# Conditioning rows in pieces as large as a pass, in places of their own, and weights in three raw buffers

## The chip, the cores and the metric

One core of a Trainium2 chip runs the whole kernel. The metric is the time of one execution on the device in microseconds (us). Engines are named as in the profile: PE is TensorE (matmuls), DVE is VectorE, ACT is ScalarE, POOL is GpSimd, SP is SyncE, which only issues DMAs here.

## What is computed

One decoder layer for 256 tokens of width 2048 in float32: a SwiGLU feed-forward, a pair of token mixers side by side (chunkwise retention and sliding-window attention), a second SwiGLU, and a final norm. Each of the three parts is modulated by nine vectors that come from one conditioning row `c`:

```python
c_act = jax.nn.silu(c)
for l in range(DEPTH):
    mod = (c_act @ w_ada[l] + b_ada[l]).reshape(b, N_MOD, D_MODEL)
    h = modulate(rms_norm(x, norm_ffn1[l]), mod[:, 0], mod[:, 1])
    x = x + 0.5 * mod[:, 2][:, None, :] * swiglu(h, w_ffn1_gu[l], w_ffn1_down[l])
    h = modulate(rms_norm(x, norm_mix[l]), mod[:, 3], mod[:, 4])
    x = x + mod[:, 5][:, None, :] * token_mixing(h, w_in[l], ...)
    h = modulate(rms_norm(x, norm_ffn2[l]), mod[:, 6], mod[:, 7])
    x = x + 0.5 * mod[:, 8][:, None, :] * swiglu(h, w_ffn2_gu[l], w_ffn2_down[l])
return rms_norm(x, norm_final)
```

The change concerns how `w_ada` (9 x 2048 rows of 2048 numbers, transposed on the host) is read, and how the large weights share buffers with it.

## The kernel before

**Weights.** Every product is made of three TensorE passes on split operands. A weight tile (`raw`, 128 x 4 x 512, 1 MB) is loaded by SyncE (`load`, line 348). Each half of it, 128 x 1024 numbers, is cast by ScalarE to the high part `wh` (line 373), and VectorE writes the remainder `wl` (line 374). Both turn in three buffers (`wsp`). A half feeds twelve matmuls (lines 365 to 367): two slices of the contraction, two halves of the tokens, three products each. In the down products and the branch products the activations are split on the fly as well (`a`, lines 405 and 406). The pool `raws` has four buffers (`RAWS`).

**Conditioning.** The nine vectors are not made on TensorE, except for the first columns: VectorE multiplies a row of `w_ada` (128 x 2048, 1 MB) by `cact` and sums along the row (`ada_pass`, line 244). Such a pass covers a part of the row. Three sets run in the shadow of the products: the first (vectors 2, 4 and 3) beside the end of the first feed-forward, two passes of 1024 for each of 48 rows; the second (7, 6 and 5) beside the mixers, four passes of 512 for each of 48 rows; the third (8) beside the second feed-forward, four passes for each of 16 rows.

**What sets the order.** `conditioning` (line 283) is a generator; `tick`, called once after the products of each half (line 423), moves it on by the rate that `set_pace` worked out (for the second set 192 steps over 262 - 8 halves). A row is loaded whole, when the step two ahead of its first pass is reached. In the first set it goes into one of two places in a slot (`two_rows`); in the second and third it takes one of the four raw buffers (`raw_row`), beside the weights. SyncE's instructions stand in the order in which the program is written, and it works them off one after another, so a load that waits for its buffer holds those behind it. On TensorE, VectorE and ScalarE a scheduler sets the order from the program's priorities and its own model of time, except in a few stretches that are written out by hand: the start, and the ends of the three down products (`down_product`, line 642) with the norm that follows.

Of the kernel before, what the change touches and what calls it, by code (L numbers as in the profile page):

```python
# [10 lines left out]
F32 = mybir.dt.float32  # L11
# [6 lines left out]
P = 128  # L18
S = 256
D = 2048  # L20
DFF = 5632
NT = S // P
KD = D // P
KF = DFF // P
CH = 512
KB = 4
EPS = 1e-6
RAWS = 4
# [50 lines left out]
def layer_kernel(  # L79
# [23 lines left out]
    nc = tc.nc  # L103
    ctx.enter_context(tc.manual_schedule(engines={mybir.EngineType.SP}))
    b_ada = b_ada[0]
    one = ctx.enter_context(tc.tile_pool(name="one", bufs=1))
    raws = ctx.enter_context(tc.tile_pool(name="raws", bufs=RAWS))
    wsp = ctx.enter_context(tc.tile_pool(name="wsp", bufs=3))
    asp = ctx.enter_context(tc.tile_pool(name="asp", bufs=2))
    slots = ctx.enter_context(tc.tile_pool(name="slots", bufs=4))  # L110
# [9 lines left out]
    def nm(s):  # L120
        uid[0] += 1
        return f"{s}_{uid[0]}"
# [15 lines left out]

    def slot():
        return slots.tile([P, KD * S], F32, tag="slot", name=nm("slot"))  # L140

    def small(n, tag):
        return two.tile([P, n], F32, tag=tag, name=nm(tag))
# [88 lines left out]
    AQ = 4  # L232
    LEAD = 3

    def ada_load(m, k, w, loads=1):
        src = w_ada[(m * KD + k) * P : (m * KD + k + 1) * P, :]
        for i in range(loads):
            at = slice(i * D // loads, (i + 1) * D // loads)
            nc.sync.dma_start(w[:, at], src[:, at])

    def ada_pass(k, w, sums, q, passes=AQ):

        at = slice(q * D // passes, (q + 1) * D // passes)
        nc.vector.tensor_tensor_reduce(  # L244
            out=w[:, at],
            in0=w[:, at],
            in1=cact[:, at],
            scale=1.0,
            scalar=0.0,
            op0=ALU.mult,  # L250
            op1=ALU.add,
            accum_out=sums[:, k, q : q + 1],
        )

    def ada_sums():
        return two.tile([P, KD, AQ], F32, tag="sums", name=nm("sums"))

    def ada_end(m, ks, sums, i=None, passes=AQ):

        dest, total = modc[:, m, ks], sums[:, ks, 0]  # L260
        if passes > 1:
            total = dest
            nc.vector.tensor_reduce(out=dest, in_=sums[:, ks, :passes], axis=AX.X, op=ALU.add)
        nc.vector.tensor_add(dest, total, bcols[:, m, ks])
        if i is not None:
            nc.vector.tensor_mul(dest, dest, gains[:, i, ks])

    def raw_row():
        raw = raws.tile([P, KB, CH], F32, tag="raw", name=nm("raw"))
        return raw.rearrange("p k n -> p (k n)")  # L270

    def two_rows():

        both = slot()
        turn = [both[:, :D], both[:, D:]]

        def place():
            turn.append(turn.pop(0))
            return turn[-1]

        return place

    def conditioning(outputs, place, ahead, passes):


        tiles = [(m, k) for m, _, _ in outputs for k in range(KD)]
        held = {}
        step = 0
        for m, gain, row in outputs:
            sums = ada_sums()  # L290
            for k in range(KD):
                for q in range(passes):
                    for i in range(step // passes, min((step + ahead) // passes + 1, len(tiles))):
                        if i not in held:
                            held[i] = place()
                            ada_load(*tiles[i], held[i])
                    ada_pass(k, held[step // passes], sums, q, passes)
                    step += 1
                    if k == KD - 1 and q == passes - 1:
                        ada_end(m, slice(0, KD), sums, gain, passes)  # L300
                        if row is not None:
                            gate_out(m, row)
                    yield

    def gate_out(m, row):

        ps = bank()
        nc.tensor.transpose(ps[:KD, :P], modc[:, m, :], ident)
        flat = t512()[:KD, :P]
        nc.scalar.mul(flat, ps[:KD, :P], row)  # L310
        nc.gpsimd.dma_start(gate_d[m // 3].rearrange("(k p) -> k p", p=P), flat)
# [9 lines left out]

    pace = {"steps": iter(()), "rate": 0.0, "due": 0.0}

    def set_pace(outputs, halves, place, ahead, idle=0, passes=AQ):
        assert next(pace["steps"], None) is None
        pace["steps"] = conditioning(outputs, place, ahead, passes)
        pace["rate"] = len(outputs) * KD * passes / (halves - idle)
        pace["due"] = -idle * pace["rate"]

    def tick():  # L330
# [15 lines left out]


    def load(w, kb, c0):
        raw = raws.tile([P, KB, CH], F32, tag="raw", name=nm("raw"))
        nc.sync.dma_start(  # L350
            raw,
            w[kb * KB * P : (kb + 1) * KB * P, c0 : c0 + CH].rearrange(
                "(k p) n -> p k n", p=P
            ),
        )
        return raw
# [278 lines left out]
    def ffn_up(held, w, tiles, first, bg=None, ready=None):  # L635
        for ci in range(first, DFF // CH):
            bg = bg or gemm(held, w, [ci * CH])[0]
            bu = gemm(held, w, [DFF + ci * CH], ready=ready)[0]
            swiglu_up(bg, bu, tiles, ci)
            bg = ready = None  # L640

    def down_product(act, w, gate, KT, before, after):
# [12 lines left out]
        with tc.manual_schedule(engines=ORDERED):  # L655
# [11 lines left out]
            def late_pieces(kb):  # L667
                raw, place = load(w, kb, c0s[1]), home_tile()
                for h in range(2):
                    late[kb, h] = Piece(raw, h, place, h).both()  # L670
# [175 lines left out]
    early = [ada_sums() for _ in range(2)]  # L846
    rows_of = {}
# [4 lines left out]
    def place(m, k, loads=1):  # L852
        if k < 1:
            rows_of[m, k] = raw_row()
        elif k == 2:
            rows_of[m, k] = lead_rows.pop(0)
        else:
            ring.append(ring.pop(0))
            rows_of[m, k] = ring[-1]
        if (m, k) not in by_column:  # L860
            ada_load(m, k, rows_of[m, k], loads)
            return
        src = ada_first[by_column.index((m, k))]
        for i in range(loads):
            at = slice(i * D // loads, (i + 1) * D // loads)
            nc.sync.dma_start(rows_of[m, k][:, at], src[:, at])
# [4 lines left out]
    def order_of(g):  # L871
        return chunks if (g + len(groups)) % 2 else chunks[::-1]

    def block_of(n, k0, k1):
        c0 = (n % 2) * DFF + (n // 2) * CH
        return gu[k0 * P : k1 * P, c0 : c0 + CH]

    def lead_blocks(k):
        raw = raws.tile([P, KB, CH], F32, tag="raw", name=nm("raw"))
        for i, n in enumerate(order_of(0)[:LEAD]):  # L880
            nc.sync.dma_start(raw[:, i, :], block_of(n, k, k + 1))
        return raw

    def load_blocks(n, ks):
        raw = raws.tile([P, KB, CH], F32, tag="raw", name=nm("raw"))
        nc.sync.dma_start(
            raw[:, : len(ks), :],
            block_of(n, ks[0], ks[-1] + 1).rearrange("(k p) n -> p k n", p=P),
        )
        return raw  # L890
# [7 lines left out]
    place(1, 0, 2)  # L898
    place(0, 0, 4)
    lead = [lead_blocks(0)]  # L900
    place(1, 1)
    place(0, 1, 4)
# [3 lines left out]

    def passes_of(m, k, passes):
        for q in range(passes):
            ada_pass(k, rows_of[m, k], early[m], q, passes)

    def end_of(m, ks, passes):
        ada_end(m, slice(ks[0], ks[-1] + 1), early[m], 0 if m else None, passes)
# [130 lines left out]
    coming_raws, sent = {}, [0]  # L1043
# [15 lines left out]
    with tc.manual_schedule(engines=ORDERED):  # L1059
# [28 lines left out]
        def rounds(m, k, i0=0, i1=KD):  # L1088
# [8 lines left out]
            out=s2, in_=ssq.rearrange("p (t i) -> p t i", t=NT), axis=AX.X, op=ALU.add  # L1097
        )
        nc.vector.tensor_scalar(
            out=v2, in0=s2, scalar1=1.0 / D, scalar2=EPS, op0=ALU.mult, op1=ALU.add  # L1100
# [6 lines left out]
            out=q2, in0=q2, scalar1=-0.5, scalar2=1.5, op0=ALU.mult, op1=ALU.add  # L1107
# [75 lines left out]
    turn = [acc_bank, side_bank, acc_bank]  # L1183
# [37 lines left out]
    for g, ks in enumerate(groups):  # L1221
# [7 lines left out]
        for i, n in enumerate(order):  # L1229
            if i < first_i:  # L1230
                continue
            at = i - first_i
# [11 lines left out]
                )  # L1244
    gate = gate_row()
    tiles.append(slot())
    place = two_rows()
    set_pace([(2, None, 0.5), (4, 1, None), (3, None, None)], 138, place, 2, passes=2)
    ffn_up(held, gu, tiles, EARLY)
    gate_load(gate, 2)  # L1250
    wi = w_in[0]
# [1 line left out]
    down_product(Whole(tiles), dn, gate, KF, *calls)  # L1253


    set_pace([(7, 2, None), (6, None, None), (5, None, 1.0)], 262, raw_row, 2, 8)

    def in_chunk(c0, ready=None):
        return gemm(held, wi, [c0], ready=ready)[0]
# [31 lines left out]
    both = slot()  # L1291
# [258 lines left out]
    for p in range(2):  # L1550
# [7 lines left out]
        for i in range(2):  # L1558
            for t in range(NT):
                m = sg[:, 0, i, t, :]  # L1560
# [15 lines left out]

    gate = gate_row()
    tiles = [slot() for _ in range(3)]
    set_pace([(8, None, 0.5)], 160, raw_row, 2, 8)
    ffn_up(held, w_ffn2_gu[0], tiles, 0, head, ready)  # L1580
    gf = one.tile([P, KD * S], F32, tag="hh", name="gf")[:, :D]
    nc.gpsimd.dma_start(gf, norm_final[None, :].broadcast_to([P, D]))
# [92 lines left out]
```

## Time and profile before

| | |
|---|---|
| median of three runs | 2427.44 us (2422.0 to 2429.84) |
| the profiled execution | 2424.57 us, of which the span 2422.8 us |
| PE busy | 2392.9 us, 99% of the span |
| DVE busy | 1700.2 us, 70% |
| ACT busy | 1183.1 us, 49% |
| mean of the DMA traffic | 249 GB/s |

The profiled execution is one run of its own; its time and its span differ by what lies around the first and the last instruction. A busy PE is a PE with matmuls in flight; the trace gives the start of each, and the distance of two starts is the pace. Idle time of the other engines costs nothing as long as PE does not wait for them.

### The profile page before, as it was taken

How to read it: one execution, taken by the hardware profiler on the slowest of the kernel's cores; microseconds unless marked ns; L12 is line 12 of the kernel's file. 1: busy time of each engine (PE TensorE's matmuls, PEld its weight loads, DVE VectorE, ACT ScalarE, POOL GpSimd, SP SyncE). 2: the span in 40 equal slices, each digit the busy share in tenths (PEclk: the TensorE clock that was granted, in tenths of full speed). 3: DMA queues.
4: the chain of work that ended last, by engine and by line, in shares of the span. 5: the costliest groups of instructions: out<-in, count | busy, mean ns of one | idle time of the engine just before them, and what ended most of it. 6: DMA issues, size and time to landing. Idle time of an engine off the chain costs nothing.

```text
span 2422.8 us, 29112 instructions
## 1 busy us (share of the span) xinstructions
PE 2392.9 (99%) x11019; PEld 1968.3 (81%) x11019; DVE 1700.2 (70%) x2487; ACT 1183.1 (49%) x1606; POOL 11.8 (0%) x26
## 2 busy tenths in 40 slices
PE   8999999999999999999999999999999999999998
PEld 6888888888788888778888788888888888888886
DVE  6888687778978689887666776768565555545656
ACT  6644554444546455454544444456444444444544
POOL 0000000000000000000000000000000000000000
PEclk9999999999999999999999999999999999999999
DMA  9977678888886666665677777755666666665553
GB/s 370 380 273 279 211 277 332 331 311 314 312 292 216 243 226 228 224 229 208 249 252 260 245 258 273 267 190 191 214 242 222 226 226 239 230 224 192 185 198 122
DMA packets 245503, 603.35 MB, mean 249 GB/s; under 512 B 9953, under 2 KB 10097, under 8 KB 226033
## 3 DMA queue, kind: packets, MB, share of 16 engines
q1 hardware_dynamic: 243586, 591.44, 68.7%
q0 software_dynamic: 1776, 10.04, 1.1%
q8 instruction: 86, 1.41, 0.2%
q14 instruction: 55, 0.45, 0.1%
HBM read 597.23 MB, written 4.22 MB: 248 GB/s over the span
## 4 chain that ended last, share of the span: by engine, by line
PE 96%; DVE 2%; DMA 1%; ACT 0%; issue 0%; SPq 0%; DVEq 0%; ACTq 0%
PE pa L366 29%; PE pa L367 29%; PE pa L365 29%; PE pa L741 1%; PE pd L367 1%; PE pd L365 1%; PE pd L366 1%; PE ps L483 1%; PE pd L1322 1%; PE pa L1022 0%; DVE wl L374 0%; DMA raw<-in_ada_first_dram 0%; PE pd L1388 0%; PE ps L939 0%; PE pd L1374 0%
## 5 line engine op out<-in xcount | busy, mean ns | idle before, releaser
L374 DVE TENSOR_TENSOR wl<-raw,wh 128x1024 fp32r<-128x1024 f32 (+1 forms) x784 | 941.2, 1206 | 576.1 <-ACT wh L373 575.2
L373 ACT CAST wh<-raw 128x1024 fp32r<-128x1024 f32 (+1 forms) x784 | 815.2, 1040 | 1006.8 <-PE pa L366 942.5
L365 PE MATMUL pa<-wh,hh 128*128 128x512 f32 x2012 | 786.4, 391 | 3.2 <-DVE t L1453 3.0
L366 PE MATMUL pa<-wh,hl 128*128 128x512 f32 x2012 | 785.7, 391 | 0.0
L367 PE MATMUL pa<-wl,hh 128*128 128x512 f32 x2012 | 724.2, 392 | 0.0
L365 PEld LDWEIGHTS pa<-wh,hh 128*128 128x128 f32 x2012 | 377.9, 188 | 81.9 <-ACT wh L373 4.5
L366 PEld LDWEIGHTS pa<-wh,hl 128*128 128x128 f32 x2012 | 377.8, 188 | 77.1
L367 PEld LDWEIGHTS pa<-wl,hh 128*128 128x128 f32 x2012 | 376.1, 188 | 76.1
L366 PE MATMUL pa<-wh,a 128*128 128x512 f32 x992 | 385.0, 390 | 3.3 <-DVE a L406 3.3
L365 PE MATMUL pa<-wh,a 128*128 128x512 f32 x992 | 367.9, 391 | 1.0 <-ACT wh L373 0.9
L367 PE MATMUL pa<-wl,a 128*128 128x512 f32 x992 | 367.5, 390 | 0.6 <-DVE wl L374 0.6
L366 PEld LDWEIGHTS pa<-wh,a 128*128 128x128 f32 x992 | 186.7, 188 | 43.4 <-DVE a L406 4.8
L365 PEld LDWEIGHTS pa<-wh,a 128*128 128x128 f32 x992 | 186.4, 188 | 41.6 <-ACT wh L373 1.8
L367 PEld LDWEIGHTS pa<-wl,a 128*128 128x128 f32 x992 | 186.2, 188 | 40.2 <-DVE wl L374 1.8
L244 DVE CUSTOM_DVE_ANT_0 slot<-slot,cact 128x1024 f32<-128x1024 f32 (+1 forms) x122 | 173.0, 1448 | 21.7 <-DMA slot<-in_w_ada_dram 21.4
L244 DVE CUSTOM_DVE_ANT_0 raw<-raw,cact 128x512 f32<-128x512 f32 x256 | 162.0, 688 | 29.2 <-DMA raw<-in_w_ada_dram 28.9
L406 DVE TENSOR_TENSOR a<-slot,a 128x512 fp32r<-128x512 f32 x124 | 84.7, 684 | 4.9 <-ACT a L405 4.9
L405 ACT CAST a<-slot 128x512 fp32r<-128x512 f32 x124 | 76.4, 618 | 5.3 <-PE pa L367 5.2
L365 PE MATMUL pd<-wh,hh 128*128 128x512 f32 x146 | 57.2, 392 | 0.2 <-DVE slot L1033 0.2
L366 PE MATMUL pd<-wh,hl 128*128 128x512 f32 x146 | 56.9, 390 | 0.0
L484 ACT COPY slot<-ps 128x512 f32<-128x512 f32 x68 | 37.6, 585 | 31.9 <-PE ps L483 31.7
L367 PE MATMUL pd<-wl,hh 128*128 128x512 f32 x146 | 51.9, 392 | 0.0
(261 smaller groups left out, 1388.7 us busy)
## 6 DMA issues: line engine op xcount, KB each, us to landing
raw<-in_w_ffn_gu_dram SPq DMA_DIRECT2D x148, 1024.0 KB, 4.9
raw<-in_w_in_dram SPq DMA_DIRECT2D x104, 1024.0 KB, 5.0
raw<-in_w_ffn_down_dram SPq DMA_DIRECT2D x88, 1024.0 KB, 5.2
slot<-in_w_ada_dram SPq DMA_DIRECT2D x74, 1024.0 KB, 7.8
raw<-in_w_ada_dram SPq DMA_DIRECT2D x64, 1024.0 KB, 4.9
raw<-in_w_ffn_gu_dram SPq DMA_DIRECT2D x25, 768.0 KB, 6.0
raw<-in_w_swa_branch_dram SPq DMA_DIRECT2D x16, 1024.0 KB, 5.2
raw<-in_w_ret_branch_dram SPq DMA_DIRECT2D x16, 1024.0 KB, 5.1
```

The lines of the kernel that those rows point to most:

```text
L244: nc.vector.tensor_tensor_reduce(out=w[:, at], in0=w[:, at], in1=cact[:, at], scale=1.0, scalar=0.0, op0=ALU.mult, op1=ALU.add, accum_out= ...
L365: nc.tensor.matmul(ps, ah[:, j, ts], wh[:, j, :], start=first, stop=False)
L366: nc.tensor.matmul(ps, al[:, j, ts], wh[:, j, :], start=False, stop=False)
L367: nc.tensor.matmul(ps, ah[:, j, ts], wl[:, j, :], start=False, stop=last)
L373: nc.scalar.copy(hi, src)
L374: nc.vector.tensor_sub(lo, src, hi.bitcast(F32))
L405: nc.scalar.copy(hi, v)
L406: nc.vector.tensor_sub(lo, v, hi.bitcast(F32))
L483: nc.tensor.transpose(ps[:, j * P : (j + 1) * P], src_of(j), ident)
L484: nc.any.tensor_copy(dest, ps[:, : n * P])
L741: nc.tensor.matmul(banks[t], a[:, j, t * P : (t + 1) * P], wt[:, j, :], start=(kb, hs[0], n) == (0, 0, 0), stop=(kb, hs[-1], n) == (KD // ...
L1322: nc.tensor.matmul(of_t[t][:, i, :], qs[:, t * P : (t + 1) * P], keys[:, n, kv, : (t + 1) * P], start=n == 0, stop=n == 1,)
```

## The change

A conditioning set gets a home of its own: a slot (16 KB a partition) for the first set, the buffer of a new pool `cond` for the second and third. The home is cut into places as large as a pass, four in each case (4 x 1024 and 4 x 512 numbers a row). A load brings one piece instead of a row: 512 KB in the first set, 256 KB in the others. It is issued at the step in which the place of the pass before has come free, three steps ahead of its own pass. Each set begins with two empty steps (`REST`) after its first loads.

The pool `raws` has three buffers. Until the mixers the buffer of `cond` is the fourth in the weights' turn (`raw_tile`); from then on weights have three.

```diff
-    raws = ctx.enter_context(tc.tile_pool(name="raws", bufs=RAWS))
+    raws = ctx.enter_context(tc.tile_pool(name="raws", bufs=RAWS - 1))
+    cond = ctx.enter_context(tc.tile_pool(name="cond", bufs=1))
...
+    turns = [0]
+
+    def raw_tile():
+
+        if turns[0] >= 0:
+            turns[0] += 1
+        pool = raws if turns[0] % RAWS else cond
+        return pool.tile([P, KB, CH], F32, tag="raw", name=nm("raw"))
...
-    def conditioning(outputs, place, ahead, passes):
-
-
-        tiles = [(m, k) for m, _, _ in outputs for k in range(KD)]
-        held = {}
+    REST = 2
+
+    def conditioning(outputs, home, passes):
+
+
+        n = D // passes
+        pieces = [(m, k, q) for m, _, _ in outputs for k in range(KD) for q in range(passes)]
+        rings = home.shape[1] // n
+        views = [home[:, i * n : (i + 1) * n] for i in range(rings)]
+        sent = 0
+
+        def loads(upto):
+            nonlocal sent
+            while sent < min(upto, len(pieces)):
+                m, k, q = pieces[sent]
+                row = (m * KD + k) * P
+                nc.sync.dma_start(
+                    views[sent % rings], w_ada[row : row + P, q * n : (q + 1) * n]
+                )
+                sent += 1
+
+        loads(rings)
+        for _ in range(REST):
+            yield
         step = 0
         for m, gain, row in outputs:
             sums = ada_sums()
             for k in range(KD):
                 for q in range(passes):
-                    for i in range(step // passes, min((step + ahead) // passes + 1, len(tiles))):
-                        if i not in held:
-                            held[i] = place()
-                            ada_load(*tiles[i], held[i])
-                    ada_pass(k, held[step // passes], sums, q, passes)
+                    loads(step + rings)
+                    ada_pass(k, views[step % rings], sums, q, passes)
                     step += 1
...
-        pace["rate"] = len(outputs) * KD * passes / (halves - idle)
+        pace["rate"] = (len(outputs) * KD * passes + REST) / (halves - idle)
...
     def load(w, kb, c0):
-        raw = raws.tile([P, KB, CH], F32, tag="raw", name=nm("raw"))
+        raw = raw_tile()
...
-    place = two_rows()
-    set_pace([(2, None, 0.5), (4, 1, None), (3, None, None)], 138, place, 2, passes=2)
+    set_pace([(2, None, 0.5), (4, 1, None), (3, None, None)], 138, slot(), passes=2)
...
-    set_pace([(7, 2, None), (6, None, None), (5, None, 1.0)], 262, raw_row, 2, 8)
+    turns[0] = -1
+    set_pace([(7, 2, None), (6, None, None), (5, None, 1.0)], 262, cond_row(), 8)
...
-    set_pace([(8, None, 0.5)], 160, raw_row, 2, 8)
+    set_pace([(8, None, 0.5)], 160, cond_row(), 8)
```

Line numbers move by some twenty: the remainder `wl` is line 394 after it, a pass 254, a piece load 303, a weight load 370.

VectorE at the beginning of the branch products (second set), before; `wl` are remainders, the lines on `sums` are passes and the reading of their sums, `a` is the low part of an activation:

```order
L374 TENSOR_TENSOR wl_10646<-raw_10643,wh_10645 128x1024
L244 ISA raw_10738,sums_10778<-raw_10738,cact 128x512
L244 ISA sums_10778 128x1
L244 ISA raw_10738,sums_10778<-raw_10738,cact 128x512
L244 ISA sums_10778 128x1
L244 ISA raw_10738,sums_10778<-raw_10738,cact 128x512
L244 ISA sums_10778 128x1
L244 ISA raw_10738,sums_10778<-raw_10738,cact 128x512
L244 ISA sums_10778 128x1
L374 TENSOR_TENSOR wl_10663<-raw_10643,wh_10662 128x1024
L406 TENSOR_TENSOR a_10637<-slot_6379,a_10637 128x512
L374 TENSOR_TENSOR wl_10682<-raw_10679,wh_10681 128x1024
```

and after, at the same place of the program:

```order
L394 TENSOR_TENSOR wl_10814<-raw_10793,wh_10813 128x1024
L254 ISA raw_6257,sums_10911<-raw_6257,cact 128x512
L254 ISA sums_10911 128x1
L254 ISA raw_6257,sums_10911<-raw_6257,cact 128x512
L254 ISA sums_10911 128x1
L394 TENSOR_TENSOR wl_10840<-raw_10837,wh_10839 128x1024
L426 TENSOR_TENSOR a_10831<-slot_6431,a_10831 128x512
L394 TENSOR_TENSOR wl_10858<-raw_10837,wh_10857 128x1024
L254 ISA raw_6257,sums_10911<-raw_6257,cact 128x512
L254 ISA sums_10911 128x1
L394 TENSOR_TENSOR wl_10876<-raw_10873,wh_10875 128x1024
```

Four passes of one row stood between two remainders of one tile; now one or two stand there, and more often.

SyncE at the same place, before:

```order
L350 DMA raw_10600<-in_w_swa_branch_dram 128x4x512
L239 DMA raw_10618<-in_w_ada_dram 128x2048
L350 DMA raw_10643<-in_w_swa_branch_dram 128x4x512
L350 DMA raw_10679<-in_w_swa_branch_dram 128x4x512
L350 DMA raw_10720<-in_w_swa_branch_dram 128x4x512
L239 DMA raw_10738<-in_w_ada_dram 128x2048
```

and after:

```order
L370 DMA raw_10713<-in_w_swa_branch_dram 128x4x512
L303 DMA raw_6257<-in_w_ada_dram 128x512 x2
L370 DMA raw_10757<-in_w_swa_branch_dram 128x4x512
L303 DMA raw_6257<-in_w_ada_dram 128x512
L370 DMA raw_10793<-in_w_swa_branch_dram 128x4x512
L303 DMA raw_6257<-in_w_ada_dram 128x512 x2
```

A row among every three or so weight tiles has become one or two pieces behind each.

VectorE in the first feed-forward's down product (first set), before:

```order
L374 TENSOR_TENSOR wl_4414<-raw_4411,wh_4413 128x1024
L406 TENSOR_TENSOR a_4405<-slot_144,a_4405 128x512
L244 ISA slot_2910,sums_3832<-slot_2910,cact 128x1024
L244 ISA sums_3832 128x1
L244 ISA slot_2910,sums_3832<-slot_2910,cact 128x1024
L244 ISA sums_3832 128x1
L374 TENSOR_TENSOR wl_4432<-raw_4411,wh_4431 128x1024
L374 TENSOR_TENSOR wl_4451<-raw_4448,wh_4450 128x1024
```

and after:

```order
L394 TENSOR_TENSOR wl_4443<-raw_4440,wh_4442 128x1024
L426 TENSOR_TENSOR a_4434<-slot_147,a_4434 128x512
L254 ISA slot_2913,sums_3907<-slot_2913,cact 128x1024
L254 ISA sums_3907 128x1
L394 TENSOR_TENSOR wl_4461<-raw_4440,wh_4460 128x1024
L394 TENSOR_TENSOR wl_4481<-raw_4478,wh_4480 128x1024
L254 ISA slot_2913,sums_3907<-slot_2913,cact 128x1024
L254 ISA sums_3907 128x1
```

Two passes in a run have become single passes.

## Rows read from the trace of the kernel before

**Rows 1.** The page's head and part 1: busy us, share of the span, instructions.

```profile
span 2422.8 us, 29112 instructions
PE 2392.9 (99%) x11019; PEld 1968.3 (81%) x11019; DVE 1700.2 (70%) x2487; ACT 1183.1 (49%) x1606; POOL 11.8 (0%) x26
```

**Rows 2.** The page's part 4, the chain that ended last, by engine.

```profile
PE 96%; DVE 2%; DMA 1%; ACT 0%; issue 0%; SPq 0%; DVEq 0%; ACTq 0%
```

**Rows 3.** Timeline of PE: start and length in us; in brackets the idle time.

```profile
1331.95 0.39 PE L366 MATMUL pa<-wh,a 128*128 128x512 f32 x1
1332.18 0.39 PE L367 MATMUL pa<-wl,a 128*128 128x512 f32 x1
...
1333.48 0.73 PE L365 MATMUL pa<-wh,a 128*128 128x512 f32 x2 [0.46 <-ACT wh L373]
1336.29 0.50 PE L366 MATMUL pa<-wh,a 128*128 128x512 f32 x1 [2.07 <-DVE a L406]
```

**Rows 4.** Waits of PE, whole span: us in total, times, longest us.

```profile
PE pa L366 <- DVE a L406: 3.3, 3, 2.1
PE pa L193 <- ACT c L190: 3.2, 1, 3.2
PE pa L365 <- DVE t L1453: 3.0, 2, 1.9
```

**Rows 5.** Stretches: us, then PE, PEld, DVE, ACT, POOL busy, clock, DMA, GB/s.

```profile
455.00:705.00 250.00, 247.58 (x1091) 202.35 (x1090) 205.39 (x263) 117.80 (x138) 1.63 (x3) 1.00 0.87 322
800.00:1090.00 290.00, 287.00 (x1444) 233.47 (x1444) 239.12 (x480) 152.69 (x305) 1.58 (x3) 1.00 0.65 232
1090.00:1345.00 255.00, 252.47 (x1136) 208.39 (x1135) 165.77 (x307) 119.48 (x163) 0.00 (x0) 0.99 0.68 241
...
1700.00:2110.00 410.00, 410.00 (x1846) 340.15 (x1845) 232.60 (x299) 176.99 (x190) 0.00 (x0) 1.00 0.65 230
```

**Rows 6.** Timeline of DVE from 1327 us.

```profile
1327.06 1.23 DVE L374 TENSOR_TENSOR wl<-raw,wh 128x1024 fp32r<-128x1024 f32 x1 [1.49 <-ACT wh L373]
1331.95 0.69 DVE L244 CUSTOM_DVE_ANT_0 raw<-raw,cact 128x512 f32<-128x512 f32 x1 [3.67 <-DMA raw<-in_w_ada_dram]
...
1334.41 1.22 DVE L374 TENSOR_TENSOR wl<-raw,wh 128x1024 fp32r<-128x1024 f32 x1
```

**Rows 7.** Timeline of DVE and ACT at the output projection's end.

```profile
1660.35 1.22 DVE L472 TENSOR_TENSOR wl<-raw,wh 128x1024 fp32r<-128x1024 f32 x1 [1.49 <-ACT wh L469]
...
1671.73 0.69 DVE L609 TENSOR_TENSOR t<-pa,row 128x512 f32<-128x512 f32 x1 [0.69 <-PE pa L367]
...
1665.54 1.99 ACT L469 CAST wh<-raw 128x1024 fp32r<-128x1024 f32 x2
```

**Rows 8.** Timeline of DVE in the first set.

```profile
526.79 1.23 DVE L244 CUSTOM_DVE_ANT_0 slot<-slot,cact 128x1024 f32<-128x1024 f32 x1 [1.95 <-DMA slot<-in_w_ada_dram]
...
531.94 1.22 DVE L244 CUSTOM_DVE_ANT_0 slot<-slot,cact 128x1024 f32<-128x1024 f32 x1 [0.50 <-DMA slot<-in_w_ada_dram]
```

**Rows 9.** SP: one issue in the timeline, and one line of its waits.

```profile
1325.60 0.34 SPq L239 DMA_DIRECT2D raw<-in_w_ada_dram  x1
...
SPq L350 <- DMA raw<-in_w_ada_dram: 85.2, 23, 6.7
```

**Rows 10.** DMA issues: count, KB each, median us from issue to landing.

```profile
raw<-in_w_ffn_gu_dram SPq DMA_DIRECT2D x148, 1024.0 KB, 4.9
...
slot<-in_w_ada_dram SPq DMA_DIRECT2D x74, 1024.0 KB, 7.8
...
raw<-in_w_ffn_gu_dram SPq DMA_DIRECT2D x14, 512.0 KB, 3.8
```

**Rows 11.** Waits of DVE for conditioning loads, whole span: us, times, longest.

```profile
DVE raw L244 <- DMA raw<-in_w_ada_dram: 28.9, 24, 3.7
DVE slot L244 <- DMA slot<-in_w_ada_dram: 21.4, 23, 2.2
```

More of the change, by code (lines that the diff above doesn't have):

```diff
@@ L244, in ada_pass @@
         nc.vector.tensor_tensor_reduce(
-            out=w[:, at],
-            in0=w[:, at],
+            out=w,
+            in0=w,
             in1=cact[:, at],
@@ L268, in raw_row, with cond_row @@
     def raw_row():
-        raw = raws.tile([P, KB, CH], F32, tag="raw", name=nm("raw"))
+        raw = raw_tile()
         return raw.rearrange("p k n -> p (k n)")
[L272 to L281, printed above, removed]
-    def conditioning(outputs, place, ahead, passes):
-        tiles = [(m, k) for m, _, _ in outputs for k in range(KD)]
-        held = {}
+    def cond_row():
+        return cond.tile([P, KB, CH], F32, tag="raw", name=nm("raw")).rearrange(
+            "p k n -> p (k n)"
+        )
[13 more added lines that the diff above has]
+                    views[sent % rings], w_ada[row : row + P, q * n : (q + 1) * n]
+                )
+                sent += 1
+        loads(rings)
+        for _ in range(REST):
+            yield
         step = 0
@@ L322, in layer_kernel, with set_pace @@
     pace = {"steps": iter(()), "rate": 0.0, "due": 0.0}
-    def set_pace(outputs, halves, place, ahead, idle=0, passes=AQ):
+    def set_pace(outputs, halves, home, idle=0, passes=AQ):
         assert next(pace["steps"], None) is None
-        pace["steps"] = conditioning(outputs, place, ahead, passes)
-        pace["rate"] = len(outputs) * KD * passes / (halves - idle)
+        pace["steps"] = conditioning(outputs, home, passes)
+        pace["rate"] = (len(outputs) * KD * passes + REST) / (halves - idle)
         pace["due"] = -idle * pace["rate"]
@@ L348, in load @@
     def load(w, kb, c0):
-        raw = raws.tile([P, KB, CH], F32, tag="raw", name=nm("raw"))
+        raw = raw_tile()
         nc.sync.dma_start(
@@ L878, in lead_blocks @@
     def lead_blocks(k):
-        raw = raws.tile([P, KB, CH], F32, tag="raw", name=nm("raw"))
+        raw = raw_tile()
         for i, n in enumerate(order_of(0)[:LEAD]):
@@ L884, in load_blocks @@
     def load_blocks(n, ks):
-        raw = raws.tile([P, KB, CH], F32, tag="raw", name=nm("raw"))
+        raw = raw_tile()
         nc.sync.dma_start(
@@ L908, in passes_of @@
         for q in range(passes):
-            ada_pass(k, rows_of[m, k], early[m], q, passes)
+            at = slice(q * D // passes, (q + 1) * D // passes)
+            ada_pass(k, rows_of[m, k][:, at], early[m], q, passes)
     def end_of(m, ks, passes):
```

## Prediction

> **What bounds the kernel now.** I read the page's shares first. TensorE is busy for 2392.9 of 2422.8 us, VectorE for 70% of the span [rows 1], and the chain that ended last runs through TensorE for 96% of it [rows 2]. A change to loads and to VectorE can give back only the time in which TensorE stands still. The rest, 11,019 matmuls that start 0.227 us apart (1331.95 and 1332.18 in [rows 3]), is untouched. The list of TensorE's waits says who ends them [rows 4]: one of 3.2 us is the start of the program, which the change leaves alone; the others are ended by VectorE, at L406 (the low part of an activation pair) and L1453 (rotary). The table of stretches places them [rows 5]: TensorE is idle for 2.42 us of 455 to 705, 3.0 us of 800 to 1090 and 2.53 us of 1090 to 1345. **That is the whole prize: 7.95 us, 0.33% of the span.** From 1700 to 2110, where conditioning also runs, it is idle for 0.0.
>
> Next I asked why VectorE is late there. In [rows 6] it stands at a conditioning pass (L244) until 1331.95, waiting 3.67 us for a whole row, and then does the row's four passes in a run; the weight remainder (`wl`, L374) behind them starts only at 1334.41. It had ended the one before at 1327.06 + 1.23 = 1328.29, so weights were blocked for 6.1 us. How much TensorE can bear follows from the three `wh`/`wl` buffers: one half of a weight tile is 12 matmuls, 12 x 0.227 = 2.72 us; a buffer comes free two halves (5.44 us) before its new content is due, plus two matmuls (0.45 us) since `wl` is read third; the cast takes 1.0 us [rows 7] and the remainder 1.23 us [rows 6]. **Cover: 5.9 - 2.2 = 3.7 us.** A block of 6.1 us should cost 2.4 us; TensorE lost 0.46 + 2.07 = 2.53 us [rows 3]. In the first set the same happens with two passes a row: waits of 1.95 and 0.50 us, each before two passes of 1.22 us [rows 8], and TensorE idle at 534 to 547. The stretch 455 to 705 is 87% loaded on the DMA engines, VectorE 82% (205.39 of 250) [rows 5].
>
> **The change part by part.** *Same work.* 48 rows x 2 passes and 64 rows x 4 passes were 96 + 256 passes and are 96 + 256 pieces; the passes keep their shapes (1.22 us [rows 8] and 0.69 us [rows 6]). Four PSUM copies move from ScalarE to VectorE by the scheduler; at some 0.7 us (as L609, which reads PSUM at this size [rows 7]) that is 2.8 us of VectorE work over 800 us in which it is idle for over 100: nothing.
>
> *More issues on SyncE.* 112 row loads become 352 piece loads, 240 more at 0.34 us [rows 9], so 82 us of a queue that issues about 2.4 DMAs per weight tile (0.85 us of 5.44). They are hidden by SyncE's waits for raw buffers. If that cover went, a weight load would go out 0.5 us later.
>
> *Runs of passes are split.* The order shows four passes in a row before, and one or two between remainders now; in the first set two before, one now. With a piece, a block is one wait plus one or two passes, no longer a wait plus four. This removes the two losses that I tied to rows: 2.42 us (455 to 705) and 2.53 us (1090 to 1345): **-4.95 us**. What is late next there is the wait for a piece.
>
> *The new wait.* A piece is issued behind the weight load of its turn, and SyncE holds that one until a remainder three tiles earlier is done. Reading the order with its waits: of the 256 pieces in the second and third set 26 have one remainder between that release and their pass, 212 two, 18 more; of the 96 in the first set 44 have two, 52 three. So the three steps ahead (194 steps over 254 halves are 0.76 a half, so 3 steps are 3.9 halves, 10.7 us) are not kept: one remainder is 2.72 us of TensorE's pace, two are 5.44. When does a piece land? A weight tile of 1 MB alone lands in 4.9 us, a row of 1 MB behind one in 7.8 [rows 10], so 2.9 us per MB of queue: 4.9 + 0.7 = 5.6 us for 256 KB behind a tile, 6.3 us for 512 KB (estimates; 512 KB alone in 3.8 us [rows 10] is the bound below). First set: 6.3 - 5.44 = 0.9 us of wait + 1.22 = 2.1 us blocked, under the cover of 3.7: nothing. Second set, two remainders: 0.2 + 0.7 = 0.9 us: nothing. One remainder: 5.6 - 2.72 + 0.7 = 3.6 us: just under the cover. In seven places two pieces stand behind one remainder: 6.3 - 2.72 + 0.7 = 4.3 us, 0.6 over: 7 x 0.6 = 4.2 us. Below, the 512 KB row's 3.8 us for the piece would give 0. I take **+1.5 us**, nearer to 0, since other VectorE work stands in most of these places and TensorE's stalls of today in them are already in the 2.53.
>
> VectorE's waits for DMA were 28.9 + 21.4 us in 47 places [rows 11]; after the change I expect more of them, some 60 to 90 us in over 100 places, each short. That row is not a loss by itself.
>
> *Three raw buffers.* From the mixer on weights turn in three buffers. Before, a tile was released six remainders ahead; now four: 4 x 2.72 = 10.9 us for a landing of 4.9 us and a cast: hidden with 5 us to spare. The tightest place is the end of the output projection, where tiles are split faster than TensorE takes them: the second tile of the next norm's weights would be let go when the remainder at 1660.35 ends (1661.57) and lands at 1666.5, while ScalarE casts it at 1665.54 [rows 7]: 0.9 us late, then ScalarE's squares behind it. VectorE idles 0.69 us just after, waiting for TensorE at 1671.73 [rows 7], so about 0.2 us is left. Zero in the sum; 0.9 us without that idle time. In return no weight load stands behind a row's landing any more, for which SyncE waited 85.2 us in 23 places [rows 9].
>
> *Rotary.* The 3.0 us of 800 to 1090 end at L1453 [rows 4], in VectorE work that is dense with or without conditioning (239.12 of 290 us [rows 5]). The scheduler reorders it; it may go or grow by as much. Zero, bounds -3.0 and +3.0.
>
> **Sum:** -4.95 + 1.5 = -3.45 us. The profiled execution took 2424.57 us for a span of 2422.8; the median of the runs is 2427.44. I put the difference on the median: **2424.0 us**.
>
> The trace has tiles of 1 MB, 512 KB and a row behind a tile, and the second MB of a queue costs 2.9 us, not 4.9, so the fixed part of a DMA overlaps with what is ahead of it [rows 10]. The Trainium skill (DMA: Bandwidth & Descriptors, section Bandwidth) gives a rule that speaks against this change: batch DMAs to 1 MiB or more, and its section on the anatomy of one DMA prices each at about 2.0 us plus bytes / 436 GB/s. By that price with nothing overlapping, a row in four pieces would cost 8 us of fixed time in place of 2 and one in two pieces 4, an estimate of 64 x 6 + 48 x 2 = 480 us more of DMA time, and the change would make the kernel slower by a good part of it. The trace speaks against that for loads that queue up; no row of it shows 256 KB pieces behind tiles. What of the rule may hold is rival D below, which is priced from rows alone.
>
> **The rivals.** *B, what is gained is given back by the piece waits.* For: the lead of one or two remainders, not three steps. Against: 0.9 us blocks in 212 of 256. Price: the bounds above, 4.2 in place of 1.5 and a rotary stall that grows by 1 to 2: 2426 to 2428. Chance 0.17.
>
> *C, everything goes.* For: four passes in a run stood ahead of the rotary stalls too; unprofiled runs reach 2429.84, and what widens them may be the same stalls. Price: -7.95: 2419.5. Chance 0.11.
>
> *D, slower: the piece becomes what VectorE stands at.* Place: the second set, 800 to 1345, VectorE 82% busy [rows 5]. It decides once a piece lands later than 5.7 us after its tile's release (2.72 + 3.7 - 0.7). At 6.6 us, still less than the 7.8 of [rows 10], the 12 single places lose 0.9 us and the 7 double ones 1.6: 22 us, less 4.95: 2444; half of it 2435. Against: DMA engines are 65 to 68% loaded there, so queues are short. Chance 0.12.
>
> **How the numbers follow.** Forecast 0.60, B 0.17, C 0.11, D 0.12. A measurement can tell about 0.3% (7.3 us) from no change: forecast and B are inside, C just outside below with most of its weight, D outside above; 0.02 of the forecast's spread goes to faster. Faster 0.13, same 0.75, slower 0.12. The range runs from C's end (2418, nearly all stalls gone) to the near end of D (2434).
>
> **What would show it.** Right: TensorE idle in 455 to 705 and 1090 to 1345 falls from 5 to under 2 us; VectorE's waits for pieces are more in number, under 3 us each; no weight load waits for a conditioning landing; 1700 to 2110 stays at 0. Wrong: TensorE waits for `wl` with VectorE at a pass just ahead of it (D), or new waits at the ends of the down products, where weights turn in three buffers.

## Result and the profile after

The changed kernel takes 2439.76 us (median of 6 runs, 2438.74 to 2445.06) against 2427.14 us for the kernel before (6 runs): ratio 1.006, 95% interval 1.0048 to 1.0072 (ratios are worked out from undisturbed runs and differ a little from the quotient of the medians, here 1.0052). It is slower by 0.6%; 2424.0 us with a range of 2418 to 2434 was forecast, so the time lies outside the range, on the side of rival D. The profiled execution took 2444.6 us. It is one of the two slowest of the six; the other four lie between 2438.74 and 2440.01 us. So the 20 us by which its span is longer are an upper end of the loss: the medians differ by 12.6 us.

The page's head, its part 1 and the first line of part 4 (beside [rows 1, 2]):

```profile
span 2442.8 us, 29236 instructions
...
PE 2399.3 (98%) x11019; PEld 1968.1 (81%) x11019; DVE 1710.5 (70%) x2491; ACT 1180.8 (48%) x1602; POOL 11.9 (0%) x26
...
PE 86%; DMA 7%; DVE 4%; issue 2%; ACT 0%; SPq 0%; DVEq 0%; ACTq 0%
```

The chain of waits now runs through DMA for 7% and VectorE for 4%, where it was 1% and 2%. The waits of TensorE, three lines of the list (beside [rows 4]):

```profile
PE pa L387 <- DVE wl L394: 11.5, 12, 2.6
PE pa L386 <- DVE a L426: 5.4, 7, 1.1
PE pa L385 <- DVE t L1474: 3.6, 2, 2.1
```

The first line was small in the kernel before:

```profile
PE pa L367 <- DVE wl L374: 0.6, 2, 0.4
```

TensorE now waits for weight remainders. Where does that happen? One matmul that comes once in each of the two norms inside the kernel, behind a short wait for VectorE, is a milestone. Timeline of PE, before:

```profile
772.78 0.33 PE L568 MATMUL ps<-small_c,t 128*128 128x128 f32 x1 [0.36 <-DVE t L561]
...
1684.31 0.33 PE L568 MATMUL ps<-small_c,t 128*128 128x128 f32 x1 [0.36 <-DVE t L561]
```

and after:

```profile
795.23 0.44 PE L588 MATMUL ps<-small_c,t 128*128 128x128 f32 x2 [0.36 <-DVE t L581]
...
1704.46 0.44 PE L588 MATMUL ps<-small_c,t 128*128 128x128 f32 x2 [0.37 <-DVE t L581]
```

Up to the first milestone, where the first set runs, the kernel loses 795.23 - 772.78 = 22.45 us. From there to the second, beside the second set, it takes 909.23 us in place of 911.53, which is 2.3 us less; the rest of the span is 738.5 before and 738.3 after. The 2.3 us are not clear of scatter: the runs below that load the same pieces as early in this part took 909.1 to 912.1 us for it. The stretches say the same (columns as in [rows 5]):

```profile
455.00:705.00 250.00, 237.74 (x1024) 191.26 (x1024) 193.37 (x250) 109.04 (x129) 2.13 (x4) 0.99 0.86 306
800.00:1090.00 290.00, 286.19 (x1438) 233.57 (x1437) 236.32 (x469) 148.69 (x293) 0.54 (x1) 1.00 0.61 214
1090.00:1345.00 255.00, 255.00 (x1166) 210.59 (x1165) 174.31 (x327) 123.46 (x178) 1.05 (x2) 1.00 0.72 252
1345.00:1600.00 255.00, 253.89 (x1131) 209.50 (x1130) 182.29 (x274) 121.15 (x139) 1.06 (x2) 1.00 0.76 261
```

In 455 to 705 TensorE starts 1024 matmuls where it started 1091. Its idle time there is 12.26 us, and over the whole stretch up to the first norm 16.84 us (2.42 before, the sum of its gaps from 190 us on). The other 8 us of the 22.45 are not in the column of idle time: a matmul in flight counts as busy for 0.39 us while the pace is 0.227, so a start that is late by less than the difference (0.16 us) leaves no gap, and a longer stall shows 0.16 us too short. Adding up by how much each start that comes over 0.3 us after the one before exceeds 0.227 gives 6.3 us before (36 starts) and 28.2 us after (83 starts), a difference of 21.9. The 47 more late starts hide 47 x 0.163 = 7.7 us.

VectorE's waits for conditioning loads (beside [rows 11]) and the landings (beside [rows 10]):

```profile
DVE slot L254 <- DMA slot<-in_w_ada_dram: 88.7, 53, 4.8
DVE raw L254 <- DMA raw<-in_w_ada_dram: 84.5, 114, 2.9
```

```profile
raw<-in_w_ada_dram SPq DMA_DIRECT2D x256, 256.0 KB, 5.3
slot<-in_w_ada_dram SPq DMA_DIRECT2D x96, 512.0 KB, 7.5
```

VectorE now waits for some 85 us in the first set and as much in the other two. In the second and third set (`raw`) that costs little: TensorE is idle for 0 and 1.11 us of 1090 to 1600, and not at all where the third set runs. In the first (`slot`) it costs 22 us of this execution. One round of it, first SyncE's queue, then VectorE, then TensorE, in the first feed-forward's down product:

```profile
592.75 0.38 SPq L370 DMA_DIRECT2D raw<-in_w_ffn_down_dram  x1
593.17 0.50 SPq L303 DMA_DIRECT2D slot<-in_w_ada_dram  x1
600.15 0.38 SPq L370 DMA_DIRECT2D raw<-in_w_ffn_down_dram  x1
```

```profile
589.75 1.22 DVE L254 CUSTOM_DVE_ANT_0 slot<-slot,cact 128x1024 f32<-128x1024 f32 x1 [1.21 <-DMA slot<-in_w_ada_dram]
...
591.50 1.22 DVE L394 TENSOR_TENSOR wl<-raw,wh 128x1024 fp32r<-128x1024 f32 x1
...
594.87 1.23 DVE L254 CUSTOM_DVE_ANT_0 slot<-slot,cact 128x1024 f32<-128x1024 f32 x1 [1.63 <-DMA slot<-in_w_ada_dram]
...
596.02 1.22 DVE L394 TENSOR_TENSOR wl<-raw,wh 128x1024 fp32r<-128x1024 f32 x1
...
598.90 1.22 DVE L394 TENSOR_TENSOR wl<-raw,wh 128x1024 fp32r<-128x1024 f32 x1
...
601.27 1.23 DVE L254 CUSTOM_DVE_ANT_0 slot<-slot,cact 128x1024 f32<-128x1024 f32 x1 [1.15 <-DMA slot<-in_w_ada_dram]
```

```profile
597.29 0.73 PE L387 MATMUL pa<-wl,a 128*128 128x512 f32 x2 [1.74 <-DVE wl L394]
```

The remainder at 591.50 ends at 592.7 and lets go a raw buffer; SyncE issues a weight tile at 592.75 and, behind it, a piece at 593.17. That piece is what the pass at 601.27 waits for: 8.1 us after its issue. Only two remainders, at 596.02 and 598.90, stand between. The second of them ends at 600.1, lets go the next tile (600.15), and the round begins again. No single block here is long: 1.21 + 1.22 and 1.63 + 1.23 us, both below the cover of 3.7 us that the prediction worked out. TensorE stands for 1.74 us all the same, since the cover had been used by the blocks ahead of it.

### The profile page after: what moved, and what is told of

It reads as the page before. It is cut to its first block, busy times and chain, and to the rows that moved or that the text cites. A ratio compares the mean times of both kernels' runs of the same rounds, so it can differ in the third digit from the quotient of the medians.

```text
span 2442.8 us, 29236 instructions
## 1 busy us (share of the span) xinstructions
PE 2399.3 (98%) x11019; PEld 1968.1 (81%) x11019; DVE 1710.5 (70%) x2491; ACT 1180.8 (48%) x1602; POOL 11.9 (0%) x26
## 4 chain that ended last, share of the span: by engine, by line
PE 86%; DMA 7%; DVE 4%; issue 2%; ACT 0%; SPq 0%; DVEq 0%; ACTq 0%
PE pa L387 26%; PE pa L386 26%; PE pa L385 25%; DMA slot<-in_w_ada_dram 4%; DVE wl L394 2%; DMA raw<-in_w_ada_dram 2%; PE pa L761 1%; PE pd L385 1%; PE pd L387 1%; PE pd L386 1%; PE ps L503 1%; PE pa L1043 0%; PE pd L1343 0%; DMA raw<-in_ada_first_dram 0%; DVE slot L254 0%
## 5 line engine op out<-in xcount | busy, mean ns | idle before, releaser
L393 ACT CAST wh<-raw 128x1024 fp32r<-128x1024 f32 (+1 forms) x784 | 814.8, 1040 | 1044.3 <-PE pa L386 971.0
L254 DVE CUSTOM_DVE_ANT_0 slot<-slot,cact 128x1024 f32<-128x1024 f32 (+1 forms) x122 | 176.5, 1449 | 88.9 <-DMA slot<-in_w_ada_dram 88.7
L254 DVE CUSTOM_DVE_ANT_0 raw<-raw,cact 128x512 f32<-128x512 f32 x256 | 174.2, 691 | 88.8 <-DMA raw<-in_w_ada_dram 84.5
L492 DVE TENSOR_TENSOR wl<-raw,wh 128x1024 fp32r<-128x1024 f32 x34 | 41.4, 1223 | 14.0 <-ACT wh L489 13.4
```

Of the source, the lines that this page charges most:

```text
L254: nc.vector.tensor_tensor_reduce(out=w, in0=w, in1=cact[:, at], scale=1.0, scalar=0.0, op0=ALU.mult, op1=ALU.add, accum_out=sums[:, k, q : ...
L393: nc.scalar.copy(hi, src)
L492: nc.vector.tensor_sub(self.lo, self.src, self.hi.bitcast(F32))
```

## Experiments

Theory L: the first set loses because its pieces have too short a lead (two or three remainders) for a landing of 7.5 us, and VectorE stands at the pass. Rivals: three raw buffers, or the mixers' pieces (B3, which is not the prediction's rival B); the load on the DMA engines and SyncE's queue as such (Q). All ratios are against the kernel before on the same chip (2423 to 2424 us there). The cuts show the lines that matter; `...` marks what is left out.

**Which set.** The change with the first set in whole rows again (by the generator of before), and the kernel before with the first set alone in pieces:

```diff
-    set_pace([(2, None, 0.5), (4, 1, None), (3, None, None)], 138, slot(), passes=2)
...
+    pace["steps"] = conditioning_rows(first, two_rows(), 2, 2)
...
```

> The change, but its first set (beside the end of the first feed-forward) is read in whole rows into two places again, as in the kernel before; the second and third set stay in pieces, and weights keep three raw buffers from the mixers on. Theory L (the loss lies in the first set, where passes stand only two or three remainders behind the release of their piece): TensorE idle between 190 and 740 us back to 2 to 3 us from 17, time 2423 to 2427 us, a little under the kernel before. Rival B3 (three raw buffers, or the pieces beside the mixers): 2437 to 2442, and the idle time between 190 and 740 does not matter.

```diff
-    set_pace([(2, None, 0.5), (4, 1, None), (3, None, None)], 138, place, 2, passes=2)
...
+    pace["steps"] = conditioning_pieces(first, slot(), 2)
...
```

> The kernel before, with pieces in the first set alone; second and third set read whole rows from the four raw buffers. Theory L: 2438 to 2445, TensorE idle between 190 and 740 us 14 to 20 us, and the stall of some 2.5 us in the branch products still there. Rival B3: 2425 to 2429.

Measured: first set in rows 2423.26 us, ratio 0.9993 (0.9984 to 1.0003), with 2.93 us of TensorE's idle time up to the first norm; first set alone in pieces 2444.47 us, 1.0082 (1.0067 to 1.0097), with 87.4 us of VectorE's waits and 15.57 us of idle time. The whole loss is in the first set. Three raw buffers and the pieces of the other two sets together cost nothing, and bring nothing that can be measured: rival B3 is out.

**Without the wait.** All pieces are loaded, into three places, but the passes of the first set multiply a resident tile and write to the fourth place, so vectors 2, 4 and 3 are not computed:

```diff
-        rings = home.shape[1] // n
+        rings = home.shape[1] // n - (passes == 2)
...
-                    ada_pass(k, views[step % rings], sums, q, passes)
+                    if passes == 2:
+                        ada_pass(k, home[:, 3 * n :], sums, q, passes, cact[:, :n])
...
```

> The change, with the passes of the first set reading a resident tile (the activated conditioning row) in place of their piece, so vectors 2, 4 and 3 are not computed; all pieces are still loaded, into three places. The passes are as long and as many, the DMA traffic is the same, and no pass waits for a DMA. Theory L (VectorE's waits for pieces are the loss): TensorE idle between 190 and 740 under 2 us, time 2419 to 2423. Rival Q (the number and size of DMAs, or their turn in SyncE's queue, makes the weight loads late): 2435 to 2445 as with the change, with TensorE waiting for casts or remainders that wait for weight loads.

Measured: 2416.68 us, ratio 0.997 (0.9959 to 0.9981), below the 2419 to 2423 us that were expected; TensorE is idle for 0.46 us of 455 to 705. The same number of bytes, issues and passes costs nothing once VectorE need not stand at a piece. The order is not the same, though: the scheduler, no longer bound by the loads, put the passes closer together, from 312 to 543 us (in the change from 326 to 724). The densest stretch of this run:

```profile
300.00:545.00 245.00, 244.54 (x1115) 202.64 (x1114) 233.71 (x320) 111.13 (x125) 2.13 (x4) 1.00 0.87 309
```

VectorE works for 95% of it and TensorE is idle for 0.46 us, so a busy VectorE alone does not hold TensorE up. Of Q only the landing is left, and the runs that follow keep the passes bound to their pieces.

**Lead.** The change with a first-set pass queued on VectorE behind the remainder that stands seven (then nine) halves earlier in the program (`splits` lists the remainders), so that more of them lie between release and pass:

```diff
+                    if passes == 2 and len(splits) >= BACK:
+                        with tc.issue_after(splits[-BACK].ins):
+                            ada_pass(k, views[step % rings], sums, q, passes)
...
```

> The change, with one thing added in the first set: a pass is queued on VectorE behind the remainder that was traced seven halves earlier, which puts five or six remainders between the release of a piece and its pass in place of two or three. Loads, pieces, places and passes are the same. Theory L: VectorE's waits for the pieces of the first set fall from 88.7 us to under 15, TensorE idle between 190 and 740 to under 3 us, time 2418 to 2424. Rival Q: 2435 to 2445. Rival P (pieces need more places): no gain, since there are still four.

> The changed kernel with a pass of the first set queued on VectorE no earlier than behind the ninth remainder before it in the program, so that 43 pieces have three and 52 four remainders between the release that lets them be issued and their pass (the change: two and three; the seventh, run before: five and six). If what counts is lead against landing, three remainders are 8.2 us against 0.5 + 7.5 = 8.0: waits of VectorE for pieces of the first set fall from 88.7 to under 20 us, TensorE idles under 4 us up to the first norm, 2420 to 2424. If a small lead of any size costs in proportion, half of the 22 us stays: about 2430.

Measured: behind the seventh 2421.62 us, ratio 0.9991 (0.9982 to 1.0); behind the ninth 2421.55 us, 0.9985 (0.9976 to 0.9994). VectorE's waits for the first set, seventh and then ninth:

```profile
DVE slot L254 <- DMA slot<-in_w_ada_dram: 0.6, 2, 0.4
```

```profile
DVE slot L254 <- DMA slot<-in_w_ada_dram: 13.3, 19, 1.4
```

With two and three remainders 88.7 us, with three and four 13.3, with five and six 0.6. These three points look like a threshold: one remainder more (2.72 us) takes away the loss, where in proportion it would have left about half. The trace of the change says the same piece by piece: counted from the release of the weight load in front, the 44 passes with two remainders have 78.9 us of the waits, the 52 with three 9.5.

**Where the piece is issued, and in how many places.** First-set pieces from GpSimd's queue, no longer behind weight loads; and three places in place of four:

```diff
-                nc.sync.dma_start(
+                (nc.gpsimd if passes == 2 else nc.sync).dma_start(
```

> The changed kernel with the first set's pieces issued from the queue of the otherwise idle GpSimd, so that a piece waits only for its own place and not behind a weight load that waits for its raw buffer; order of VectorE as in the change. If the short lead comes from standing behind the weight loads: pieces go out some four passes ahead (about 15 us), waits of the first set fall from 88.7 to under 15 us, TensorE idles under 4 us up to the first norm, 2419 to 2424. If it comes from the size of the pieces or the load of the DMA engines (87 per cent in 455 to 705), a piece still lands late wherever it is issued: waits over 50 us, 2432 or more.

```diff
-        rings = home.shape[1] // n
+        rings = home.shape[1] // n - (passes == 2)
```

> The changed kernel with three places in place of four in the first set, so that a piece is issued two steps ahead of its pass; in VectorE's order 46 pieces have two and 56 three remainders between release and pass (with four places 44 and 52 of the 96 after the start). If the lead is set by the remainder that releases the weight load in front and not by the places, nothing changes: VectorE's waits for pieces of the first set 80 to 100 us, time within 4 us of the change (2436 to 2444). If steps ahead are what buys time, waits rise over 120 us and the time over 2446.

Measured: from GpSimd 2421.37 us, ratio 0.9992 (0.9983 to 1.0001). The pieces' landing, and VectorE's waits for it:

```profile
slot<-in_w_ada_dram POOLq DMA_DIRECT2D x96, 512.0 KB, 7.0
```

```profile
DVE slot L254 <- DMA slot<-in_w_ada_dram: 3.5, 6, 1.1
```

The pieces still need 7.0 us, so size and traffic are not what hurts; they set out earlier, and most passes have four or five remainders behind the issue. The order of VectorE was expected to stay that of the change and did not: the scheduler put the passes between 315 and 627 us. So this run alone doesn't separate the queue from the order; the runs on lead do. Three places gave 2443.61 us, ratio 1.008 (1.0063 to 1.0098), with waits of 90.6 us: a step less ahead changes nothing to speak of. The lead is set by the weight load in front, not by the places.

**How the waits reach TensorE.** The change with half the sum in each first-set pass (512 of 1024 numbers; vectors 2, 4 and 3 are half sums):

```diff
-                    ada_pass(k, views[step % rings], sums, q, passes)
+                    if passes == 2:
+                        ada_pass(k, views[step % rings][:, :CH], sums, q, 4)
...
```

> The changed kernel, but each pass of the first set sums only the first 512 of its 1024 numbers, so vectors 2, 4 and 3 are not the layer's; loads, places and order stay. VectorE has 96 x (1.22 - 0.69) = 51 us less to do there. Two readings of how the waits for pieces become TensorE's idle time (16.8 us up to the first norm). Theory A, VectorE runs out of spare time: waits (88.7 us) and work together exceed the stretch; with 51 us less work the waits stay near 90 us and TensorE idles under 4 us there: 2420 to 2426. Theory B, a loop of latency: a remainder releases a weight load, the piece behind it lands 8 us later, its pass lets only two or three remainders go (5.4 to 8.2 us of TensorE's pace) before the next one waits in the same way; less work then only makes VectorE wait longer (waits near 88.7 + 51 = 140 us) and TensorE still idles 8 us or more: 2431 or more.

Measured: 2429.74 us, ratio 1.002 (1.0011 to 1.0029), TensorE idle for 5.62 us up to the first norm. Neither theory came out whole. The stretch 455 to 705 of this run, and VectorE's waits in its whole span:

```profile
455.00:705.00 250.00, 244.38 (x1067) 197.29 (x1066) 167.19 (x257) 114.82 (x135) 1.64 (x3) 1.00 0.90 321
```

```profile
DVE slot L254 <- DMA slot<-in_w_ada_dram: 118.9, 65, 4.1
```

Of 51 us of work taken from VectorE 30 became waiting, as in a loop of latency; TensorE's idle time fell by 11 us and the span by 15, as where VectorE lacks time. A reading that fits, but that no run isolates, is that both hold: the loop makes the waits, and beside them a VectorE that works for 77% (193.37 of 250) can't catch up after one, while at 67% it mostly can. The share of work alone is not it: without the wait, TensorE kept its pace beside a VectorE at 95%.

**Late passes in all sets, with pieces and with rows.** The same edit for every pass, in the change and, with whole rows and four raw buffers, in the kernel before:

```diff
+                    if len(splits) >= BACK:
+                        with tc.issue_after(splits[-BACK].ins):
+                            ada_pass(k, held[step // passes], sums, q, passes)
...
```

> As the run with passes behind the seventh remainder, but in all three sets. In the second and third set 184 of 256 pieces then have three or four remainders between release and pass (26 had one, 212 two). If waits for pieces are what is left of TensorE's losses beside the branch products (1.1 us) and the rotary part (3.6 us), waits on raw fall from 114 to under 40 us and the time to 2417 to 2420. If those losses come from elsewhere (VectorE's dense rotary work, casts), it stays at 2420 to 2423.

> The kernel before, with whole rows and four raw buffers, but every conditioning pass queued on VectorE no earlier than behind the seventh remainder before it in the program. Rows of the first set then have three or four remainders (10 and 42 of 74) between the release that lets them be issued and their first pass (before: 39 three, 20 four). If the gain of the run with late passes in all sets (ratio 0.998) needs pieces, this one stays at that of before: ratio 0.999 to 1.001, waits on slot and raw over 25 us together. If the late order alone gives it, the ratio is 0.998 or less, TensorE's idle time of 455 to 705 and 1090 to 1345 falls from 5 to under 2 us.

Measured: with pieces 2418.34 us, ratio 0.9976 (0.9967 to 0.9985); with rows 2419.5 us, 0.9984 (0.9975 to 0.9993). Both beat both kernels. VectorE's waits with pieces:

```profile
DVE raw L254 <- DMA raw<-in_w_ada_dram: 1.9, 3, 0.7
DVE slot L254 <- DMA slot<-in_w_ada_dram: 1.4, 3, 0.9
```

and with rows, with the stretch 455 to 705:

```profile
DVE raw L244 <- DMA raw<-in_w_ada_dram: 14.9, 20, 2.2
DVE slot L244 <- DMA slot<-in_w_ada_dram: 3.2, 3, 2.0
```

```profile
455.00:705.00 250.00, 249.60 (x1109) 205.94 (x1108) 207.12 (x265) 118.63 (x140) 2.13 (x4) 1.00 0.91 325
```

With rows TensorE idles for 0.40 us of 455 to 705 and 0.48 us of 1090 to 1345 (2.42 and 2.53 before). The late order alone gives most of the gain; the intervals overlap, so whether pieces add to it stays open. With pieces, late passes in all sets reach 0.9976 and in the first set alone 0.9991. So waits in the later sets may cost some 0.15% (3.6 us); these intervals overlap too, and it is not shown.

## Why the prediction was wrong, step by step

- **The bound and the prize** came out near in number and wrong in kind. With late passes in all sets the span falls to 2415.6 us, 7.2 under 2422.8 (5.8 us by the ratio), beside a prize of 7.95 us of idle time. But of those 7.95 us this run still has 1.47 + 3.08 + 0.19 + 0.21 = 4.95 (455 to 705, 800 to 1090, 1090 to 1345, 1345 to 1600). Most of the gain is in TensorE's busy time, 4.5 us less than the 2392.9 of [rows 1]:

```profile
PE 2388.4 (99%) x11019; PEld 1968.4 (81%) x11019; DVE 1703.7 (71%) x2488; ACT 1180.8 (49%) x1605; POOL 11.8 (0%) x26
```

  Late starts without a gap are time that can be given back too (6.3 us of late starts up to the first norm before, 2.42 of them seen as idle). Idle time was no upper bound, and that the two numbers are close is luck.
- **The new wait, first set: the step that failed.** It set one block (6.3 - 5.44 = 0.9 us of wait and a pass of 1.22) against a cover of 3.7 us and put the first set's waits at nothing; they cost 22 us of the profiled execution. Two things were wrong. The landing was 7.5 us, not 6.3, and from the release 0.4 us more; so with two remainders the wait is 7.9 - 5.4 = 2.5 us, with three none, if remainders keep TensorE's pace. That alone would not have changed the sum: 2.5 + 1.22 = 3.7 us is a block just at the cover. The second fault is that the cover is a stock and not an allowance for each block. It is filled again only by VectorE's spare time, and that was to be had from [rows 5]: 250 - 205.39 = 44.6 us in 455 to 705. Of 60 passes there, 44 in 96 have two remainders, some 28; at 0.9 us of wait that is 25 us and fits, at 2.5 us it is 70 and doesn't (an estimate from these counts; measured, the 44 waited 1.8 us each). By this count both faults were needed. VectorE's waits in that stretch, before and now, are

```profile
DVE wl L374 <- ACT wh L373: 25.9, 30, 1.9
DVE slot L244 <- DMA slot<-in_w_ada_dram: 17.9, 17, 2.2
...
DVE slot L254 <- DMA slot<-in_w_ada_dram: 48.4, 29, 4.8
DVE wl L394 <- ACT wh L393: 7.9, 14, 1.5
```

  A wait for a cast is the sign that VectorE is ahead and has time to spare, since the casts themselves wait for TensorE to free a `wh` (971.0 us in the span). It fell from 25.9 to 7.9 us; with late passes in the first set (behind the seventh remainder) it is 41.2. Work (193.37), waits for pieces and waits for casts fill the 250 us of the change, and TensorE did in them 1024 matmuls in place of 1091. The prediction spoke of 82% for VectorE in this stretch and didn't set the sum of the waits against it. The sum is not a fixed sum either: with less work it grew (118.9 us with half passes).
- **Rival D** had the mechanism (VectorE stands at the piece) and the wrong set. That its price (22 us less 4.95; 2435 to 2444) comes near the 22.45 us of the first set is luck: it was added up from 19 places of the second set. Its sign, TensorE waiting for `wl` with VectorE at a pass just ahead, is what the trace shows. It was put where single remainders stand, in 800 to 1345, and against it stood that queues are short there. They are: 256 KB land in 5.3 us (5.6 estimated), 5.7 from the release, hardly over the two remainders (5.44 us) that 212 pieces have. The 82% that it gave VectorE holds for 800 to 1090 alone: of 1090 to 1345 VectorE is busy for 65% before and 68% after, and the 84.5 us of waits in 114 places cost TensorE little.
- **Runs of passes split, -4.95 us:** the half of the first set was swallowed by the loss. The branch products' 2.53 us became 1.11 (a stall at 1357 in place of 1333 to 1336); with rows there (first set alone in pieces) it is 2.38. So rather more than half of this part came.
- **VectorE's waits, 60 to 90 us in over 100 places:** 173.2 us in 167; in the later sets alone 84.5 in 114, each under 3 us, as forecast; the first set's, up to 4.8 us, were not expected, and they are a loss by themselves.
- **Three raw buffers, 0:** held (0.9993 with three buffers and the first set in rows). **Rotary, 0:** its 3.0 us became 3.6, and TensorE's idle time of 800 to 1090 3.81; in the other runs with early passes and pieces there it is 2.73 to 5.38, so it more likely grew than fell, as rival B had it. **Issues on SyncE, 0:** held, no weight load waits for a conditioning landing any more, and the run without the wait issued them all.
- **The landing behind a tile.** The 7.8 us of [rows 10] that 2.9 us per MB came from are a median over 74 rows, 26 of which are loaded at the start of the program. The rows of the later sets, of 1 MB as well and from the same queue, land in 4.9 us (64 of them). So the 6.3 us for 512 KB rested on a mixture; measured in 455 to 705 it was 8.1 us for a row and is 7.5 for a piece.
- **The rule on batching.** The Trainium skill (DMA: Bandwidth & Descriptors, section Anatomy of one DMA) prices a transfer at about 2.0 us plus its bytes / 436 GB/s, a fit to loads that GpSimd issues. Behind a tile of 4.9 us with nothing overlapping that makes an estimate of 8.1 us for 512 KB and 7.5 for 256 KB. The trace has 7.5 and 5.3: in the busier first set it is nearer to the rule than to the 6.3 of the prediction, in the second it is not. Whether a fixed part or the busier DMA engines (86% of 455 to 705, 72% of 1090 to 1345) make the 7.5 us no run separates. The prediction was right that the DMA time of smaller pieces as such costs nothing (the runs without the wait and with late passes load the same pieces).

## What to carry to other kernels

A load issued behind another in an in-order queue has the lead of what releases the one in front, whatever number of buffers it has of its own: count in the order what the consuming engine does between that release and the use, and set it against the landing behind a transfer. Judge many short waits by their sum against the spare time of the engine in that stretch, not each against a cover, and look at how long that engine still waits for the one it feeds: when that time goes, it has none to spare. Where buffers are there, a later place for the consumer is a remedy that leaves the loads as they are: late passes gave 0.9984 with whole rows, the smaller loads alone 1.006. And take the idle time of TensorE for less than what it loses: here late starts that the idle column doesn't show added half as much again.

## What was not expected of the hardware

Half the bytes hardly land sooner behind a tile. Landings of 455 to 705, before and after, where the DMA engines are busy for 87 and 86%:

```profile
slot<-in_w_ada_dram SPq DMA_DIRECT2D x30, 1024.0 KB, 8.1
...
slot<-in_w_ada_dram SPq DMA_DIRECT2D x60, 512.0 KB, 7.5
```

And a busy share can hide a loss: TensorE's busy time rose by 6.4 us (2392.9 to 2399.3) with the same 11,019 matmuls, since a late start after a matmul in flight counts as busy time and not as a gap.
